# A two-layer diffusion block on one core: later loads at the start, value products of attention in threes, and one sum moved inside a scan

## The chip, the core and the metric

The kernel runs on one core of a Trainium2 chip, as one program. Its engines have a queue of instructions each and meet by semaphores: TensorE (PE, with its weight loads shown as PEld), VectorE (DVE), ScalarE (ACT), GpSimd (POOL) and SyncE (SP), which issues the DMAs. The metric is the device time of one execution in microseconds (us); the median of 3 runs before the change is 2692.45 us (2690.4 to 2694.46).

## The reference, cut to what matters

Two layers work on 2048 latent tokens of width 1024, with 256 context tokens as a prefix. Each layer's input is modulated by a shift and a scale that come from a conditioning vector:

```
mod = (silu_c @ w_ada[l] + b_ada[l])[:, None, :]
q, k, v, g_a, xb, b_g, c_g, g_b = split_cols(modulate(x, shift, scale) @ w_in, widths)   # layer 0
q, zf, zb, i, g = split_cols(modulate(x, shift, scale) @ w_in, widths)                    # layer 1
```

Layer 0 has windowed attention (8 query heads on 2 key heads; a block of 128 queries sees all 256 context keys and the 384 latent keys around it, and a sink) beside a gated short convolution:

```
p = jax.nn.softmax(jnp.concatenate([sink_l, s_ctx, s_loc], axis=-1), axis=-1)
return (jnp.einsum('bkgij,bjkd->bikgd', p[..., 1:1 + lc], vc)
        + jnp.einsum('bkgij,bjkd->bikgd', p[..., 1 + lc:], v_n))
```

Layer 1 is a gated linear recurrence in two directions, 8 heads, computed in chunks:

```
S_t = diag(f_t) S_{t-1} + k_t v_t^T ,   o_t = S_t^T q_t
```

All is float32; the products of the projections are made of two halves, a rounded one and the rest, three matmuls for each block of 128 rows of the weight.

## The kernel before, in words

**Projections.** `proj` (L370) makes one block of 128 output channels for a group of 256 or 512 tokens: 8 steps of three matmuls (L377 to L379), each with a weight tile of 128 x 128 of its own and 256 or 512 columns. Layer 0 goes over the tokens in three passes. In each, `emit` takes the blocks one after another; a block's weights come by `wload` (L282), which loads 512 KB into one of three buffers `w`, and are split into two halves on ACT (L252) and DVE (L255). At the first pass the halves are also written back to memory for the later passes.

**The start.** Before any projection the modulation of layer 0 is made by `ada` (L179): 16 loads of 512 KB into the six buffers `wh`, each followed by four matmuls that fill a quarter of the array's columns each (L190). The inputs are transposed on PE (L313). Two blocks, the keys' and the values', are worked off as soon as each quarter of the modulation is there; their weights are loaded among the modulation's (`first_w`, L570). When the values' block is done, `ab_rest` (L596) asks for the mask and sink tables and queues the transposes of the other tokens (`transposed`, L355). A scheduler orders the whole program: each engine's queue is made from the instructions' dependences and its own clock, so an instruction may come much earlier in a queue than its line. `issue_after` gives a load an earlier instruction that it has to follow in the queue.

**Attention.** It is side work, `attend` (L792), put between the projections' matmuls. For a unit of one or two query blocks it makes the scores, the softmax, and then the products with the values: the probabilities are transposed on PE (L886) into a PSUM bank `pm`, ACT copies a bank into a buffer `pt` (L888), and matmuls that fill 64 of the 128 columns each, one half for each of two heads (L894), add them up in one bank `pa`. There are two banks `pm` and four buffers `pt`. A bank takes two blocks of 128 queries for each head, so a unit of two query blocks needs five banks; L876 takes them two at a time: two banks of transposes, their products, two more, their products, the fifth, its products.

**The scan.** Layer 1's `levels` (L1193) makes a head's scores by doubling the block length: seven levels, in each a copy of the keys on ACT (L1236), matmuls that fill 32 columns each (L1279), and products on DVE (L1242, L1245). Before the first level, eight matmuls against a constant 0/1 pattern (L1220, 32 columns each too) sum the products within pairs of neighbours, from an array that DVE has made (L1207 to L1211), and ACT copies the result (L1223). There are three PSUM banks `ps` for scores and levels.

A `yield` with a number gives the side work's cost; `Side.step` spends a budget on it in proportion to the projections.

Of the kernel before, what the change touches and what calls it, by code (L numbers as in the profile page):

```python
# [21 lines left out]
ALU = mybir.AluOpType  # L22
# [3 lines left out]
P = 128  # L26
# [28 lines left out]
class Kern:  # L55
# [226 lines left out]
    def wload(self, v, tag="wh", bank="pj", key=None):  # L282
        if key in self.kept:
            return self.wback(key)[0] + (bank,)
        raw = self.t("w", [P, KC, P])
        self.last = self.nc.sync.dma_start(raw, v)
        if tag != "pt":
            hl = self.split(raw, tag=tag)
            if key is not None:
                self.wkeep(key, hl)  # L290
            return hl + (bank,)

        q = [self.split(raw[:, i:i + 4, :], (P, 4, P), tag) for i in (0, 4)]
        return Halves(*[x[0] for x in q]), Halves(*[x[1] for x in q]), bank
# [301 lines left out]
    def ab_rest(self):  # L596

        with self.tc.issue_after(self.last.ins):
            self.tables_ab()
        self.shared = True  # L600
        self.first = self.last
        for t in range(4, NT):
            self.side.add(self.transposed(self.io["x"][0, t * P:(t + 1) * P, :], self.xT[:, :, (t - 4) * P:(t - 3) * P]))
# [69 lines left out]
    def wcols(self, a, *to, key=None):  # L673
        return self.wload(self.io["w_in_ab"][a // P], *to, key=key)
# [117 lines left out]
    def attend(self, b, ts, qv, sv):  # L792
# [83 lines left out]
        for b0 in range(0, len(banks), 2):  # L876
            todo = []
            for bank in banks[b0:b0 + 2]:
# [12 lines left out]
            for s, q0, d, o, n in todo:  # L891
# [301 lines left out]
    def levels(self, r, scores):  # L1193
# [8 lines left out]
        if scores:  # L1202
# [7 lines left out]
            nc.vector.tensor_tensor(own, own, q, ALU.mult)  # L1210
# [3 lines left out]


            Sd = self.t("Sd", [P, nt, 32])
            ps = self.ps("ps")
            for row in range(2):
                for j in range(0, P, 32):
                    nc.tensor.matmul(ps[j:j + 32, :n // 4], self.alt[:, row:row + 32],  # L1220
                                     cap(on, row * n + j, [(P, nt), (2, 16), (n + 1 - 2 * row * n, 2)]),
                                     start=(row == 0), stop=(row == 1))
            nc.scalar.copy(Sd, ps[:, :n // 4].rearrange("p (i t) -> p i t", t=32))  # L1223
            Sc = self.t("Sc", [P, n])
            r["A"], r["Sc"] = A, Sc
            yield 1.0
# [4 lines left out]
        for li, m in enumerate(LEVELS):  # L1231
            nb = n // (2 * m)
            if scores and li:

                X = self.t("X", [P, n])
                nc.scalar.copy(cap(X, 0, [(2 * m, nb), (m, 2), (1, m)]), cap(K, 0, [(2 * m, nb), (n + m, 2), (1, m)]))  # L1236
                self.level(m, X, A, Sd, Sc)
# [23 lines left out]
        r["T"] = td  # L1261

# [423 lines left out]
```

## Time and profile before

| what | value |
|---|---|
| median of 3 runs | 2692.45 us |
| profiled execution | 2695.45 us, of which the span from its first to its last instruction is 2693.7 us |
| PE busy | 2648.5 us (98%), 21556 matmuls |
| PEld busy | 2228.5 us (83%) |
| DVE, ACT, POOL busy | 1665.1, 1232.3, 43.1 us |
| DMA | 427.39 MB, mean 159 GB/s |
| mean granted TensorE clock | 0.993 |
| chain that ended last, by engine | PE 93%, DMA 3%, DVE 2%, ACT 1% |

PE is busy nearly all the time. Busy is not the same as useful: the ends of matmuls are modelled, and a matmul that is shown at 0.28 us can be followed by the next after 0.12 us. What a matmul costs is the distance from its start to the next one's start, and this is how the rows of the timeline are read below.

### The profile page before, as it was taken

Reading aid. Unit: us, or ns where it says so; the run is one execution under the profiler, and the core shown is the slowest. Engines: PE = TensorE matmul, PEld = TensorE weight load, DVE = VectorE, ACT = ScalarE, POOL = GpSimd, SP = SyncE. Lnnn points to the kernel's source line nnn. Section 1 sums busy time; section 2 is a strip of 40 time slices with the busy share of each in tenths; the row PEclk is TensorE's granted clock in tenths of the full one; section 3 lists DMA queues with packets and bytes.
Section 4 is the critical chain, followed back from the end, with each engine's and each line's share of the span. In section 5 each row is a group of like instructions: output and inputs, shape, how many; then the busy total and the mean of one; then the engine's idle time right before and its main releaser. Section 6 shows DMA issues by size and latency. Waiting matters only on the chain.

```text
span 2693.7 us, 53732 instructions
## 1 busy us (share of the span) xinstructions
PE 2648.5 (98%) x21556; PEld 2228.5 (83%) x21556; DVE 1665.1 (62%) x4075; ACT 1232.3 (46%) x2827; POOL 43.1 (2%) x160
## 2 busy tenths in 40 slices
PE   8999999999999999999999999999999999999998
PEld 5978888888888878889888888888978888887786
DVE  5556664455445467788756565658666555566776
ACT  4555544446455562136544444445344445444300
POOL 0000000000000000000000000000000000000000
PEclk8999999999999999999999999999999999999999
DMA  8955544334333346655543443435344432335433
GB/s 333 314 190 182 199 166 139 118 126 144 136 131 136 114 150 193 202 166 188 181 162 137 146 153 119 157 131 183 142 167 146 154 107 103 126 111 197 147 141 110
DMA packets 201620, 427.39 MB, mean 159 GB/s; under 512 B 15910, under 2 KB 93467, under 8 KB 201371
## 3 DMA queue, kind: packets, MB, share of 16 engines
q1 hardware_dynamic: 201370, 423.96, 45.8%
q8 instruction: 170, 2.79, 0.4%
q14 instruction: 80, 0.65, 0.1%
HBM read 278.13 MB, written 145.76 MB: 157 GB/s over the span
## 4 chain that ended last, share of the span: by engine, by line
PE 93%; DMA 3%; DVE 2%; ACT 1%; issue 0%; SPq 0%; DVEq 0%; ACTq 0%
PE pj L377 17%; PE pj L378 17%; PE pj L379 17%; PE pj L505 4%; PE pj L507 4%; PE pj L506 4%; PE pa L894 3%; PE pm L886 3%; PE pm L1384 3%; PE pj L1145 2%; PE pj L1146 2%; PE pj L1144 2%; PE ps L1279 2%; PE ps L1309 2%; PE pm L1298 1%; PE ps L1220 1%
## 5 line engine op out<-in xcount | busy, mean ns | idle before, releaser
L377 PE MATMUL pj<-xa,wh 128*128 128x512 f32 x1120 | 444.3, 397 | 0.3 <-ACT gl L1130 0.3
L378 PE MATMUL pj<-xa,wh 128*128 128x512 f32 x1120 | 443.9, 396 | 0.0
L379 PE MATMUL pj<-xa,wh 128*128 128x512 f32 x1120 | 442.3, 395 | 0.0
L379 PEld LDWEIGHTS pj<-xa,wh 128*128 128x128 f32 x1120 | 210.6, 188 | 44.1 <-issue 2.5
L378 PEld LDWEIGHTS pj<-xa,wh 128*128 128x128 f32 x1120 | 210.8, 188 | 41.5 <-issue 2.7
L377 PEld LDWEIGHTS pj<-xa,wh 128*128 128x128 f32 x1120 | 210.6, 188 | 41.4 <-issue 0.9
L1236 ACT COPY X<-gl 128x512 f32<-128x512 f32 x192 | 115.4, 631 | 149.0 <-PE ps L1279 80.0
L377 PE MATMUL pj<-xb,wh 128*128 128x256 f32 x608 | 175.6, 289 | 0.7 <-ACT acc L237 0.7
L378 PE MATMUL pj<-xb,wh 128*128 128x256 f32 x608 | 174.1, 286 | 0.0
L379 PE MATMUL pj<-xb,wh 128*128 128x256 f32 x608 | 174.1, 286 | 0.0
L255 DVE TENSOR_TENSOR wh<-w,wh 128x1024 fp32r<-128x1024 f32 x98 | 119.7, 1221 | 66.6 <-ACT wh L252 57.5
L888 ACT COPY pt<-pm 128x512 f32<-128x512 f32 (+1 forms) x168 | 91.9, 579 | 142.8 <-PE pm L886 142.3
L1242 DVE TENSOR_TENSOR gl<-gl,xb 128x512 f32<-128x512 f32 (+1 forms) x240 | 149.0, 632 | 7.8 <-ACT X L1236 6.3
L1245 DVE TENSOR_TENSOR A<-A,xb 128x512 f32<-128x512 f32 x192 | 131.2, 686 | 33.6 <-PE ps L1279 33.1
L252 ACT CAST wh<-w 128x1024 fp32r<-128x1024 f32 x98 | 102.1, 1049 | 107.1 <-PE pj L378 81.2
L377 PE MATMUL pj<-kb,wh 128*128 128x512 f32 (+1 forms) x384 | 140.0, 365 | 3.9 <-ACT gl L1130 3.4
L378 PE MATMUL pj<-kb,wh 128*128 128x512 f32 (+1 forms) x384 | 138.9, 362 | 0.0
L497 ACT CAST wh<-wh 128x1024 fp32r<-128x1024 f32 (+2 forms) x36 | 35.9, 997 | 224.7 <-DMA wh<-yT_ab 98.1
L379 PE MATMUL pj<-kb,wh 128*128 128x512 f32 (+1 forms) x384 | 138.3, 360 | 0.0
L826 DVE CUSTOM_DVE_ANT_0 ps<-ps,am,c_sink 128x384 f32<-128x384 f32 (+1 forms) x128 | 76.6, 603 | 93.4 <-PE ps L823 80.4
L377 PEld LDWEIGHTS pj<-xb,wh 128*128 128x128 f32 x608 | 115.8, 190 | 5.9 <-issue 2.7
L837 ACT ACTIVATE p<-ps,sm 128x256 f32<-128x256 f32 x144 | 68.3, 475 | 109.0 <-DVE sm L834 105.7
(384 smaller groups left out, 6553.1 us busy)
## 6 DMA issues: line engine op xcount, KB each, us to landing
wh<-w_parts SPq DMA_DIRECT2D x180, 512.0 KB
w_parts<-wh SPq DMA_DIRECT2D x148, 512.0 KB
w<-in_w_in_c SPq DMA_DIRECT2D x48, 512.0 KB
w<-in_w_ada SPq DMA_DIRECT2D x32, 512.0 KB
w<-in_w_in_ab SPq DMA_DIRECT2D x28, 512.0 KB
wh<-yT_ab SPq DMA_DIRECT2D x18, 512.0 KB
w<-x1T SPq DMA_DIRECT2D x18, 512.0 KB
wh<-in_w_ada SPq DMA_DIRECT2D x16, 512.0 KB
```

What stands on the lines that cost most here:

```text
L252: nc.scalar.copy(hi, raw)
L255: e.tensor_tensor(lo, raw, hi[:].bitcast(F32), ALU.subtract)
L377: nc.tensor.matmul(p[:, :N], hi[:, k, :], xh, start=(k == 0), stop=False)
L378: nc.tensor.matmul(p[:, :N], hi[:, k, :], xl, start=False, stop=False)
L379: nc.tensor.matmul(p[:, :N], lo[:, k, :], xh, start=False, stop=(k == KC - 1))
L505: nc.tensor.matmul(p, r["hi"][:, k, :], wh[:, s], start=(k == 0), stop=False)
L506: nc.tensor.matmul(p, r["hi"][:, k, :], wl[:, s], start=False, stop=False)
L507: nc.tensor.matmul(p, r["lo"][:, k, :], wh[:, s], start=False, stop=(k == KC - 1))
L888: nc.scalar.copy(d[:, :, 0:o], pt.rearrange("p (h c) -> p h c", h=2)[:, :, 0:o])
L1236: nc.scalar.copy(cap(X, 0, [(2 * m, nb), (m, 2), (1, m)]), cap(K, 0, [(2 * m, nb), (n + m, 2), (1, m)]))
L1242: nc.vector.tensor_tensor(kk, kk, cap(pt_, po + 1, [(pd - 1, 2), (2, nb), (0, m)]), ALU.mult)
L1245: nc.vector.tensor_tensor(aa, aa, cap(pt_, po + pd + 1, [(-pd - 1, 2), (2, nb), (0, m)]), ALU.mult)
```

## The change

It has three parts. The loads of weights for blocks other than the first two, the tables and the first token loads are held behind the last load of the modulation. Attention takes its banks three at a time instead of two, and goes through their products in reversed order, the last transposed first. In the scan the sums within pairs, and the DVE product that they need, move into the step of the first scored level.

```
-    def wload(self, v, tag="wh", bank="pj", key=None):
+    def wload(self, v, tag="wh", bank="pj", key=None, after=None):
...
-        self.last = self.nc.sync.dma_start(raw, v)
+        with self.tc.issue_after(after.ins) if after else ExitStack():
+            self.last = self.nc.sync.dma_start(raw, v)
...
     def ab_rest(self):
-        with self.tc.issue_after(self.last.ins):
+        with self.tc.issue_after(self.ada_last.ins):
             self.tables_ab()
         self.shared = True
-        self.first = self.last
+        self.first = self.ada_last
...
     def wcols(self, a, *to, key=None):
-        return self.wload(self.io["w_in_ab"][a // P], *to, key=key)
+        return self.wload(self.io["w_in_ab"][a // P], *to, key=key, after=None if to else self.ada_last)
...
-        for b0 in range(0, len(banks), 2):
+        for b0 in range(0, len(banks), 3):
             todo = []
-            for bank in banks[b0:b0 + 2]:
+            for bank in banks[b0:b0 + 3]:
...
-            for s, q0, d, o, n in todo:
+            assert not first or (todo[-1][1] == 0 and todo[-1][4] == nt * P)
+            for s, q0, d, o, n in reversed(todo):
...
-            nc.vector.tensor_tensor(own, own, q, ALU.mult)
...
-            ps = self.ps("ps")
-            for row in range(2):
-                for j in range(0, P, 32):
-                    nc.tensor.matmul(ps[j:j + 32, :n // 4], self.alt[:, row:row + 32],
...
-            nc.scalar.copy(Sd, ps[:, :n // 4].rearrange("p (i t) -> p i t", t=32))
...
-            yield 1.0
...
                 nc.scalar.copy(cap(X, 0, [(2 * m, nb), (m, 2), (1, m)]), cap(K, 0, [(2 * m, nb), (n + m, 2), (1, m)]))
+                if li == 1:
+                    nc.vector.tensor_tensor(own, own, q, ALU.mult)
+                    self.within(on, Sd)
                 self.level(m, X, A, Sd, Sc)
...
+    def within(self, on, Sd):
+        nc = self.nc
+        n = on.shape[-1]
+        nt = n // P
+        ps = self.ps("ps")
+        for row in range(2):
+            for j in range(0, P, 32):
+                nc.tensor.matmul(ps[j:j + 32, :n // 4], self.alt[:, row:row + 32],
+                                 cap(on, row * n + j, [(P, nt), (2, 16), (n + 1 - 2 * row * n, 2)]),
+                                 start=(row == 0), stop=(row == 1))
+        nc.scalar.copy(Sd, ps[:, :n // 4].rearrange("p (i t) -> p i t", t=32))
```

Where it moves instructions, the queues show it. First PE's queue in layer 0's attention, before: `pa_1925` is the accumulator of one unit, `pt_` its copied banks, `pj_` a projection that runs beside it.

```order
L377 MATMUL pj_2127<-xa_247,wh_2087 128x512
L894 MATMUL pa_1925<-pt_1927,vc_548 64x256 x2
L886 MATMUL pm_1944<-c_ident,p_1784 128x128
L894 MATMUL pa_1925<-pt_1934,v_582 64x256 x2
L886 MATMUL pm_1944<-c_ident,p_1784 128x128
L886 MATMUL pm_1944<-c_ident,p_1785 128x128 x2
L886 MATMUL pm_1985<-c_ident,p_1785 128x128 x2
```

The products of the first two banks stand here, with a transpose between them. The same unit (now `pa_1897`) in PE's queue after the change:

```order
L379 MATMUL pj_2243<-xa_370,wh_2209 128x512
L897 MATMUL pa_1897<-pt_1941,v_582 64x256 x2
L897 MATMUL pa_1897<-pt_1934,v_582 64x256 x2
L897 MATMUL pa_1897<-pt_1899,vc_548 64x256 x2
L888 MATMUL pm_1958<-c_ident,p_1784 128x128 x2
L888 MATMUL pm_1958<-c_ident,p_1785 128x128 x2
L380 MATMUL pj_2243<-xa_369,wh_2211 128x512
```

Three banks' products now stand together, the last copied bank first, and nothing is between them. In the whole queue the products form 132 unbroken runs before and 68 after, of 416 instructions in both. (The profile counts each of these float32 matmuls twice, so 832, and a row with x2 here is a row with x4 there.)

The second place is SP's queue in the start, before: `wh_` are the modulation's loads, `w_` weights of later blocks, `kb_588` tokens, `cs_` tables of the rotation.

```order
L188 DMA wh_334<-in_w_ada 128x1024
L286 DMA w_621<-in_w_in_ab 128x1024
L188 DMA wh_343<-in_w_ada 128x1024
L360 DMA kb_588<-in_x 128x1024
L188 DMA wh_349<-in_w_ada 128x1024
L286 DMA w_742<-in_w_in_ab 128x1024
L286 DMA w_850<-in_w_in_ab 128x1024
L188 DMA wh_382<-in_w_ada 128x1024
L188 DMA wh_388<-in_w_ada 128x1024
L188 DMA wh_397<-in_w_ada 128x1024
L188 DMA wh_403<-in_w_ada 128x1024
L683 DMA cs_495<-in_k_cos 128x512
```

After the change, SP's queue from the same load on:

```order
L188 DMA wh_334<-in_w_ada 128x1024
L188 DMA wh_343<-in_w_ada 128x1024
L188 DMA wh_349<-in_w_ada 128x1024
L188 DMA wh_382<-in_w_ada 128x1024
L188 DMA wh_388<-in_w_ada 128x1024
L188 DMA wh_397<-in_w_ada 128x1024
L188 DMA wh_403<-in_w_ada 128x1024
L685 DMA cs_495<-in_k_cos 128x512
L686 DMA cs_496<-in_k_sin 128x512
L164 DMA am_584<-in_k_amask 128x384
L166 DMA c_sink<-in_sink_ab 128x8
L361 DMA kb_588<-in_x 128x1024
```

Three weight loads, one token load and the two tables have moved behind the modulation's last load; `w_621`, `w_742` and `w_850` follow right behind these rows.

The third place is PE's queue in the scan, one pair of a head's two token groups, before: `kst_` holds the products to be summed, `A_` and `X_` are a level's operands.

```order
L1144 MATMUL pj_15207<-wh_15199,xa_12137 128x256
L1220 MATMUL ps_15112<-kst_15098,c_alt 32x128 x8
L1145 MATMUL pj_15207<-wh_15201,xa_12137 128x256
L1146 MATMUL pj_15207<-wh_15199,xa_12138 128x256
L1144 MATMUL pj_15207<-wh_15199,xa_12137 128x256
```

The same sum after the change (L1147 to L1149 are the values' projections, L1267 the sums, L1288 a level):

```order
L1147 MATMUL pj_15230<-wh_15222,xa_12137 128x256
L1267 MATMUL ps_15122<-kst_15098,c_alt 32x128 x8
L1288 MATMUL ps_15132<-A_15100,X_15119 32x32 x16
L1148 MATMUL pj_15230<-wh_15224,xa_12137 128x256
L1149 MATMUL pj_15230<-wh_15222,xa_12138 128x256
```

The sum that stood alone is now followed by the first level of its token group. Over the whole queue, sums and levels together form 131 unbroken runs before and 132 after.

## Rows read from the trace of the kernel before

**Rows 1.** Windows: PE, PEld, DVE, ACT, POOL busy us (instructions); clock; DMA share, GB/s
```profile
0.00:26.80 26.80, 15.98 (x111) 9.21 (x111) 9.89 (x29) 7.23 (x12) 0.83 (x9) 0.92 0.90 342
26.80:60.70 33.90, 32.67 (x209) 24.01 (x210) 23.01 (x50) 16.84 (x29) 0.00 (x0) 0.86 0.91 343
60.70:943.00 882.30, 879.96 (x5585) 734.61 (x5585) 469.94 (x1248) 462.22 (x1134) 23.34 (x79) 1.00 0.47 162
```
**Rows 2.** Timeline, PE, one run of four value products: start us, us, what, shapes
```profile
208.85 0.28 PE L377 MATMUL pj<-xb,wh 128*128 128x256 f32 x1
208.97 0.28 PE L378 MATMUL pj<-xb,wh 128*128 128x256 f32 x1
209.18 0.65 PE L894 MATMUL pa<-pt,vc 128*64 128x256 f32 x4
209.77 0.38 PE L379 MATMUL pj<-xb,wh 128*128 128x256 f32 x1
209.99 0.28 PE L377 MATMUL pj<-xb,wh 128*128 128x256 f32 x1
```
**Rows 3.** Timeline, PE, one run of eight value products
```profile
183.48 0.28 PE L379 MATMUL pj<-xb,wh 128*128 128x256 f32 x1
183.69 1.08 PE L894 MATMUL pa<-pt,vc 128*64 128x256 f32 x8
184.71 0.39 PE L377 MATMUL pj<-xb,wh 128*128 128x256 f32 x1
184.93 0.28 PE L378 MATMUL pj<-xb,wh 128*128 128x256 f32 x1
```
**Rows 4.** Timeline, PE, four value products with transposes behind them
```profile
485.81 0.40 PE L378 MATMUL pj<-xa,wh 128*128 128x512 f32 x1
486.05 0.39 PE L379 MATMUL pj<-xa,wh 128*128 128x512 f32 x1
486.37 0.65 PE L894 MATMUL pa<-pt,vc 128*64 128x256 f32 x4
486.95 0.66 PE L886 MATMUL pm<-c_ident,p 128*128 128x128 f32 x4
487.37 0.48 PE L377 MATMUL pj<-xa,wh 128*128 128x512 f32 x1
487.68 0.40 PE L378 MATMUL pj<-xa,wh 128*128 128x512 f32 x1
```
**Rows 5.** Timeline, PE, two transposes between projections
```profile
407.09 0.38 PE L886 MATMUL pm<-c_ident,p 128*128 128x128 f32 x2
407.22 0.36 PE L377 MATMUL pj<-xb,wh 128*128 128x256 f32 x1
407.42 0.28 PE L378 MATMUL pj<-xb,wh 128*128 128x256 f32 x1
```
**Rows 6.** Waits of PE, whole span: for what; us in total, times, longest
```profile
PE pm L886 <- ACT p L855: 0.6, 2, 0.3
```
**Rows 7.** Groups by form: ACT's copy of a bank; busy us, mean ns; idle before
```profile
L888 ACT COPY pt<-pm 128x512 f32<-128x512 f32 x160 | 89.3, 589 | 137.4 <-PE pm L886 136.9
```
**Rows 8.** Line L188, the modulation's loads: who waited for them (us, times)
```profile
  PEld ps L190: 0.5, 2
```
**Rows 9.** Timeline, PE, the last wait for tokens in the start
```profile
26.76 1.54 PE L313 MATMUL pm<-c_ident,kb 128*128 128x128 f32 x6 [0.53 <-DMA kb<-in_x]
```
**Rows 10.** Timeline, SP's queue, the modulation's last four loads: start, us
```profile
29.76 7.35 SPq L188 DMA_DIRECT2D wh<-in_w_ada  x4
```
**Rows 11.** Windows of the start, columns as in rows 1
```profile
20.00:30.00 10.00, 7.23 (x38) 4.39 (x39) 4.50 (x10) 3.90 (x6) 0.00 (x0) 0.62 1.03 403
30.00:40.00 10.00, 10.00 (x59) 7.29 (x58) 6.50 (x15) 4.14 (x6) 0.00 (x0) 0.70 1.03 409
```
**Rows 12.** Lines L1210 and L1223 in the scan: ns min/median/max, first and last start
```profile
L1210 DVE TENSOR_TENSOR kst<-kst,Q x32: 674/684/693, 1320.5 to 2451.8; 128x512 f32<-128x512 f32 x32
L1223 ACT COPY Sd<-ps x32: 245/267/272, 1325.9 to 2459.2; 128x128 f32<-128x128 f32 x32
```

More of the change, by code (lines that the diff above doesn't have):

```diff
@@ L1216, in levels @@
             Sd = self.t("Sd", [P, nt, 32])
-            ps = self.ps("ps")
-            for row in range(2):
-                for j in range(0, P, 32):
-                    nc.tensor.matmul(ps[j:j + 32, :n // 4], self.alt[:, row:row + 32],
-                                     cap(on, row * n + j, [(P, nt), (2, 16), (n + 1 - 2 * row * n, 2)]),
-                                     start=(row == 0), stop=(row == 1))
-            nc.scalar.copy(Sd, ps[:, :n // 4].rearrange("p (i t) -> p i t", t=32))
             Sc = self.t("Sc", [P, n])
             r["A"], r["Sc"] = A, Sc
-            yield 1.0
         prod = (F, 0, n)
```

## The prediction

> **What bounds the kernel.** I read the page's busy shares first, then the windows by stage, then PE's timeline start by start, then the waits. PE is busy 98% of the span and makes 93% of the chain that ended last, so the time is PE's queue from end to end, and what counts is what each instruction takes from that queue. The windows [rows 1] say where PE is not full: in the first 26.8 us it works 15.98; from there to the first ordinary block at 60.7 it works 32.67 of 33.9; from 60.7 to 943 us, the stage with the attention, 879.96 of 882.3. In that stage no other engine reaches 60% and the DMA share is 0.47. So there is next to nothing to win from waits there (2.3 us in 882), and a gain can only come from PE doing the same work in fewer microseconds. PE's timeline shows where such time hides. A projection of 256 columns takes 0.12 us from start to start (208.85 to 208.97). When a run of value products comes between, the steps before and behind it are longer [rows 2]: 208.97 to 209.18 is 0.21, and 209.77 to 209.99 is 0.22. That is time shown as busy in which PE does no more work.
>
> **Part 1: attention in threes.** No instruction is added or removed: PE's queue has the same 832 value products and 656 transposes, ACT the same 168 copies. What changes is how they stand together: 132 unbroken runs of value products before, 68 after. Two causes: by the code there were 100 groups (three for each of 28 two-block latent units, two for each of four units of one block with three banks, one for each of eight others) and now there are 68; and before, the scheduler slid transposes or projections into groups 32 times, for which the reversed order leaves no room, because the first product of a group now needs its last copy.
>
> The price of a run. Four products [rows 2]: from 208.97 to 209.99 is 1.02 us, less two ordinary steps of 0.12, so 0.78 us. Eight products [rows 3]: from 183.48 to 184.93 is 1.45, less 0.24, so 1.21 us. Two runs of four cost 1.56, one of eight 1.21: joining saves 0.35 us. With transposes behind the run [rows 4]: 486.05 to 487.68 is 1.63, less two projection steps of 0.24 (485.81 to 486.05) and four transposes; a pair of transposes between projections costs 0.33 less one step of 0.12 [rows 5], so 0.21, and four 0.42. That leaves 0.73 for the four products, 0.05 less than in rows 2, so I put joining there at 0.30 (an estimate: it takes the same 0.05 off the fixed part). In the new queue 43 of the 68 runs have transposes behind them. I take 0.32, with 0.30 and 0.35 as ends: 64 x 0.32 = 20.5 us, ends 19.2 and 22.4. All of it lies on the path, since the stage is PE's from start to end. The transposes themselves may be spread among the projections, as they now are more often, at no cost: the 0.21 us of a pair [rows 5] is just two steps of 0.105.
>
> What is added is a wait. The first product of a group stands in PE's in-order queue behind nothing but its semaphore, and needs the copy made last; the third bank's transposes need a bank `pm` back, of which there are two. A copy takes 589 ns [rows 7]. Behind a waiting product stands everything on PE. In the new queue 30 or so projections stand between a group's last transposes and its first product, which at 0.12 to 0.23 us each is some 4 to 6 us, ten times a copy. In the trace PE's transposes waited 0.6 us in all [rows 6] with the same two banks, and the products do not appear among the waits. I put this wait at 0, its bounds at -0.6 (those waits gone) and, were every one of the 68 groups to wait a whole copy, +40 us; I take the value of the row.
>
> The Trainium skill has two rules here that disagree. "TensorE: Matmul & The Clock Gate" (Part 2, What happens when you issue a matmul) says that one matmul's drain overlaps the next one's fill, so that a step costs just its columns; "TensorEngine Tiling (Array Packing)" (Tiling Modes, Key Properties) says that changing the tiling mode drains the engine. By the first alone joining runs would save nothing and the sum would be the start's term alone; by the second each of the 64 runs that go is a drain on the way in and one on the way out, without a price. The 0.09 and 0.10 us that the neighbours of a run lose [rows 2] side with the second.
>
> **Part 2: loads behind the modulation.** On SP six loads and two small ones move behind the modulation's last. Of the loads, four of 512 KB and the mask table of 192 KB stood between modulation loads. At the 403 to 409 GB/s of this stretch [rows 11], 2.29 MB are 5.6 us: that is what the last modulation load could gain if DMA set its time. It does not: from 26.8 us on PE is full, and in the whole start it waited for modulation weights 0.5 us, in two pieces [rows 8]; there are six buffers `wh`, so the later loads wait themselves for PE to free one, and SP spends 7.35 us on the last four [rows 10]. PE's order up to the first ordinary block is nearly the same before and after. The one wait for DMA that shows late, 0.53 us for tokens [rows 9], has the mask table ahead of it in the queue: 192 KB, 0.5 us earlier. With what PE idles up to 60.7 us (1.2 us behind 26.8, [rows 1]) I take -1 us, bounds 0 and -5.6. The moved weights are not needed before the first ordinary block at 60.7 us; all that moved is 2.3 MB more behind the last modulation load, issued by 37.1 [rows 10], so they land by about 46 (an estimate from the same rate) and are split on ACT and DVE by 50.
>
> TensorE's clock is at 1.2 GHz for part of 20 to 40 us, after PE had idled (0.62 and 0.70 of full speed over these two windows, [rows 11]): 20 us at a mean of 0.66 is about 13.6 us at half speed. The work in it can start half a microsecond earlier, no more, so I leave the loss as it is and put 2 us either way into the range.
>
> **Part 3: sums in the first scores' step.** PE's count is the same, and the runs of narrow matmuls in the scan are 131 before and 132 after: 22 sums now touch a level where 16 did, but more levels stand alone. One run more is +0.3 us by the price above. On DVE the product (684 ns) and on ACT the copy of the sums (267 ns) move from before the first level to its second step [rows 12], 32 times; PE is full there and other work covers them. Only where the last heads' levels are exposed, at the ends of the two passes (three pairs), could the 0.95 us show: 3 x 0.95 = 2.9 us, on either side, since the chain loses at its start what it gets later. I take +0.3.
>
> **Sum.** -20.5 - 1 + 0.3 = -21.2 us. The profiled execution took 2695.45 us (2693.7 in the span, 1.75 around it) and would take 2674.2; it was 3.0 us above the median of the runs, so by the median 2692.45 - 21.2 = 2671.2 us. I say 2671.
>
> What else moves: each joined group gives back 0.8 of side budget and each scan 1.0, so the side work runs a little ahead. The queue shows little of it: the last value product stands behind 3812 of 10560 projection matmuls, before behind 3931. The boundaries between stages, where PE waits now, are dealt anew; I put 5 us either way into the range for that.
>
> **Rivals.**
> 1. The start is DMA's after all: if the modulation's last load comes 5.6 us earlier and all behind it follows, the start gives 5.6 instead of 1, and the time is 2666. For it: the DMA share in the start is 0.90 or more [rows 1]. Against it: the 0.5 us of waits [rows 8]. 10%.
> 2. The new wait (slower): PE stops at groups until ACT has copied the last bank, with every projection behind. It decides from 21.2 / 68 = 0.31 us a group on; at a whole copy of 0.589 us it is 40 us, and 2692.45 - 21.2 + 40 = 2711. For it: the reversed order asks for the newest copy first, and ACT has casts of 1 us in its queue. Against it: 30 projections in between. 5%.
> 3. Joining is free of gain: if the lost steps around a run are only drawn longer, nothing changes but the start: 2691. It is what the first of the two rules above gives (the Trainium skill, "TensorE: Matmul & The Clock Gate", Part 2). For it: ends of matmuls are modelled. Against it: I use starts alone, and two timeline places agree. 4%.
> 4. Half of the gain returns as waits at 68 joined groups or at the stage boundaries: 2681. For it: denser side work asks ACT for its copies in shorter time. 6%.
>
> My forecast has the remaining 75%.
>
> **How the numbers follow.** The likeliest case's own range is -19.2 to -22.4 for the runs, 0 to -2 for the start, 0 to +3 for the scan, 5 us of boundaries and 2 of clock: about 2664 to 2678. The range that should hold 8 in 10 reaches to rival 1 below and rival 4 above: 2662 to 2682. A measurement of this kernel can tell about 0.2%, 5.4 us, from no change. Faster by more: the forecast, rivals 1 and 4, less a little for rerolled boundaries, 0.90. Within: rival 3 and small parts of the others, 0.05. Slower: rival 2, 0.05.
>
> **What would show it.** In the changed kernel's profile: busy PE in the attention's stage down by some 20 us with the same count of instructions (so the windows of that stage end some 20 us earlier), not less idle time; runs of 8 and 16 value products in PE's timeline with one long step before and one behind; the first ordinary block starting at about 59.7 us instead of 60.7; the scan's stage as long as before. Wrong would be: waits of PE for L890 (the copy of a bank) of some microseconds; the first ordinary block at 56 us or earlier; an attention stage as long as before.

## The result, and the profile after

| | before | changed |
|---|---|---|
| median of the runs | 2693.45 us (4 runs, 2690.4 to 2698.88) | 2665.94 us (4 runs, 2662.65 to 2669.1) |
| ratio, 95% interval | | 0.9896 [0.9874, 0.9917] |
| profiled execution, span | 2695.45, 2693.7 us | 2669.1, 2667.3 us |
| PE busy | 2648.5 us | 2624.7 us |
| unbroken runs of value products | 132 | 68 |

The kernel became 27.5 us faster, where 21.2 were forecast. Run once more, in another set of runs, it stood at 0.9901 [0.9887, 0.9914], which is 26.7 us. The time, 2666, lies inside the range and 5 us under the number. One of the six runs of the sums alone, below, took 8005 us at full clock for no cause that is known; its median counts that run, its ratio does not.

To see where it went I cut PE's queue at the same work in each kernel: the start (up to the first ordinary block), the middle (from there through the first 4704 ordinary projection matmuls: the attention and the output that follows it) and the rest (the scan and all behind it). The last lines of the table are the parts run alone, told below.

| span of PE, us | start | middle | rest | last matmul ends |
|---|---|---|---|---|
| before | 60.7 | 1175.5 | 1448.0 | 2684.2 |
| changed | 57.4 | 1162.5 | 1438.0 | 2657.9 |
| changed, run again | 58.1 | 1158.5 | 1440.0 | 2656.6 |
| threes alone | 58.7 | 1158.5 | 1448.9 | 2666.1 |
| sums alone | 58.0 | 1174.8 | 1439.0 | 2671.8 |
| loads alone | 58.6 | 1174.1 | 1448.1 | 2680.8 |

The middle gave 13 to 17 us, the rest 8 to 10, the start 3. The two profiles of the changed kernel differ by 4 us in the middle: TensorE was at half speed there for 13.7 us in the first and for 6.8 in the second, which makes 3.4 of the 4. The windows at these cuts show what kind of time went. First before, the middle and the rest (columns as in [rows 1]):

```profile
60.73:1236.21 1175.48, 1166.69 (x7107) 972.11 (x7106) 693.84 (x1758) 572.48 (x1337) 23.34 (x79) 1.00 0.50 167
1236.21:2684.24 1448.03, 1433.12 (x14134) 1223.12 (x14132) 932.47 (x2223) 635.75 (x1450) 18.90 (x72) 1.00 0.42 145
```

The changed kernel, the same work:

```profile
57.38:1219.90 1162.52, 1148.77 (x7108) 977.41 (x7107) 698.57 (x1758) 571.87 (x1337) 23.02 (x79) 0.99 0.51 170
1219.90:2657.90 1438.00, 1430.12 (x14134) 1224.60 (x14132) 928.20 (x2223) 633.27 (x1450) 26.03 (x72) 1.00 0.42 146
```

The counts of instructions are equal to within one. In the middle PE is busy 17.9 us less and idle 5.0 us more (13.75 against 8.79). In the rest it is the other way: 3.0 us less busy, and 7.0 us less idle (7.88 against 14.91). Two different things happened: in the middle the same matmuls became cheaper, behind it PE waits less.

What the new groups look like is in PE's timeline of the changed kernel, one run of 16:

```profile
405.46 0.39 PE L380 MATMUL pj<-xa,wh 128*128 128x512 f32 x1
405.68 0.39 PE L378 MATMUL pj<-xa,wh 128*128 128x512 f32 x1
406.00 1.09 PE L897 MATMUL pa<-pt,v 128*64 128x256 f32 x12
406.92 0.60 PE L897 MATMUL pa<-pt,vc 128*64 128x256 f32 x4
407.45 0.66 PE L888 MATMUL pm<-c_ident,p 128*128 128x128 f32 x4
```

One long step stands before the 16 (405.68 to 406.00, 0.32, where the one before it took 0.22), and the last four take 0.53 up to the transposes behind them (406.92 to 407.45), where four in the middle of a run take 0.43 (the 0.43 by which [rows 3] are longer than [rows 2]). Between them the products follow one another without idle time; by the single starts the rest of the price lies in the step behind the first pair of products (0.26 us where later pairs take 0.21) and in the second step behind the group (0.17 where 0.11 is usual).

PE's weight loads (PEld) show what is special at the two ends. In the kernel before, beside [rows 2]:

```profile
208.74 0.19 PEld L377 LDWEIGHTS pj<-xb,wh 128*128 128x128 f32 x1
208.86 0.19 PEld L378 LDWEIGHTS pj<-xb,wh 128*128 128x128 f32 x1
209.18 0.20 PEld L894 LDWEIGHTS pa<-pt,vc 128*64 128x64 f32 x4
209.76 0.19 PEld L379 LDWEIGHTS pj<-xb,wh 128*128 128x128 f32 x1 [0.39 <-issue]
209.87 0.19 PEld L377 LDWEIGHTS pj<-xb,wh 128*128 128x128 f32 x1
```

Among projections a step's weights are loaded while the step before it runs (208.74 for the matmul at 208.85, 208.86 for the one at 208.97). The load of the first product begins at 209.18, with the product itself, and the load of the projection behind the run at 209.76, with the matmul at 209.77. At both ends of a run no load runs ahead.

There is no wait for the copies: the changed kernel has no row of PE waiting for L890 (the copy, 588 ns as in [rows 7]), and the transposes' wait of [rows 6] is gone too. The idle time that the middle gained is in the output's stage behind the attention. PE's waits between 880 and 1110 us, changed kernel (us in total, times, longest):

```profile
PE pj L506 <- ACT ka L252: 3.6, 2, 2.1
PE pj L506 <- DVE A L520: 2.4, 1, 2.4
PE pj L506 <- DVE w L520: 0.6, 1, 0.6
```

Before, the same stage shows 0.4 us of such waits:

```profile
PE pj L505 <- DVE w L519: 0.4, 1, 0.4
```

The side work is done earlier now (the last value product starts at 985 us, before at 1034, while the first output matmul moved by 15 only), so less may be left to lie beside the casts for the output (L252) and DVE's residual sums (L520). That this exposes them is not shown: in two kernels below the last value product stands almost where it did (twos in reversed order, behind projection 3932) or still earlier than here (threes in the old order, behind 3788), and 3.0 and 2.6 us of such waits come in them.

### The profile page after: what moved, and what is told of

Same layout as the page of the kernel before. It is cut to its first block, busy times and chain, and to the rows that moved or that the text cites. A ratio compares the mean times of both kernels' runs of the same rounds, so it can differ in the third digit from the quotient of the medians.

```text
span 2667.3 us, 53718 instructions
## 1 busy us (share of the span) xinstructions
PE 2624.7 (98%) x21556; PEld 2233.5 (84%) x21556; DVE 1665.5 (62%) x4075; ACT 1229.1 (46%) x2827; POOL 49.9 (2%) x160
## 4 chain that ended last, share of the span: by engine, by line
PE 95%; DMA 3%; DVE 1%; ACT 1%; issue 0%; SPq 0%; DVEq 0%; ACTq 0%
PE pj L378 18%; PE pj L380 18%; PE pj L379 18%; PE pj L506 4%; PE pj L508 4%; PE pj L507 4%; PE pa L897 3%; PE pm L888 3%; PE pj L1147 3%; PE pj L1148 3%; PE pm L1393 3%; PE ps L1288 3%; PE pj L1149 3%; PE ps L1318 2%; PE pm L1307 1%; PE ps L1267 1%
## 5 line engine op out<-in xcount | busy, mean ns | idle before, releaser
L252 ACT CAST wh<-w 128x1024 fp32r<-128x1024 f32 x98 | 102.6, 1049 | 124.9 <-PE pj L379 96.1
L890 ACT COPY pt<-pm 128x512 f32<-128x512 f32 (+1 forms) x168 | 91.5, 578 | 120.5 <-PE pm L888 114.4
L378 PEld LDWEIGHTS pj<-xb,wh 128*128 128x128 f32 x608 | 115.9, 191 | 6.4 <-DVE sg L789 1.7
L379 PEld LDWEIGHTS pj<-xb,wh 128*128 128x128 f32 x608 | 115.9, 191 | 2.6 <-issue 1.5
```

The source lines that it names most:

```text
L252: nc.scalar.copy(hi, raw)
L378: nc.tensor.matmul(p[:, :N], hi[:, k, :], xh, start=(k == 0), stop=False)
L379: nc.tensor.matmul(p[:, :N], hi[:, k, :], xl, start=False, stop=False)
L890: nc.scalar.copy(d[:, :, 0:o], pt.rearrange("p (h c) -> p h c", h=2)[:, :, 0:o])
```

## The experiments

Each kernel is the one before with the edit shown, unless said otherwise. Times are medians of the runs, the difference is the ratio to the kernel before with its 95% interval, turned into us.

| run | median, us | ratio | against before, us |
|---|---|---|---|
| e1_threes | 2674.55 | 0.9935 [0.9922, 0.9947] | -17.5 [-21.0, -14.3] |
| e2_loads | 2692.02 | 0.9999 [0.9991, 1.0008] | -0.3 [-2.4, 2.2] |
| e3_sums | 2684.94 | 0.9968 [0.9956, 0.998] | -8.6 [-11.8, -5.4] |
| e4_threes_fwd | 2693.61 | 1.0007 [0.9998, 1.0017] | 1.9 [-0.5, 4.6] |
| e5_sums_stay | 2686.89 | 0.9981 [0.9972, 0.999] | -5.1 [-7.5, -2.7] |
| e6_sums_keep | 2689.27 | 0.9991 [0.9982, 1.0] | -2.4 [-4.8, 0] |
| e7_twos_rev | 2685.96 | 0.9974 [0.9964, 0.9984] | -7.0 [-9.7, -4.3] |
| e8_fives | 2717.16 | 1.0097 [1.0082, 1.0113] | 26.1 [22.1, 30.4] |
| e9_after_again | 2665.94 | 0.9901 [0.9887, 0.9914] | -26.7 [-30.4, -23.2] |
| e10_threes_sums | 2666.87 | 0.9905 [0.9892, 0.9919] | -25.6 [-29.1, -21.8] |
| e11_fewer_cr | 2728.05 | 1.0131 [1.0116, 1.0147] | 35.3 [31.2, 39.6] |
| e12_fives_w | 2680.21 | 0.9953 [0.9941, 0.9966] | -12.7 [-15.9, -9.2] |

**Threes alone**

```diff
-        for b0 in range(0, len(banks), 2):
+        for b0 in range(0, len(banks), 3):
-            for s, q0, d, o, n in todo:
+            for s, q0, d, o, n in reversed(todo):
```

> The kernel before with part 2 alone: attention's banks in threes, the products of a group issued in reversed order. PE's queue then has 68 unbroken runs of value products instead of 132. Theory A (each run costs PE a fixed 0.32 to 0.35 us): the stage up to the last value product ends 20 to 22 us earlier, and the whole kernel is 13 to 22 us faster, since the next stage may take back up to 7 us as idle time of PE. Rival B (the gain of the change came from the scan's and the start's parts): 0 to 5 us faster. Rival C (all parts of the 27 us hang on this one, because the boundaries behind it fall better): 25 to 30 us faster.

It came out as theory A says. Middle and rest in its windows:

```profile
58.71:1217.20 1158.49, 1145.90 (x7107) 975.34 (x7106) 696.33 (x1758) 571.93 (x1337) 23.17 (x79) 1.00 0.50 169
1217.20:2666.10 1448.90, 1435.48 (x14134) 1226.03 (x14132) 932.20 (x2223) 635.54 (x1450) 18.78 (x72) 1.00 0.42 145
```

The middle is 17.0 us shorter: 20.8 us less busy, 3.8 more idle. The rest is as long as before, so this part gains nothing in the scan, and rivals B and C are out.

**Threes in the old order**

```diff
-        for b0 in range(0, len(banks), 2):
+        for b0 in range(0, len(banks), 3):
```

> The kernel before with attention's banks in threes, but the products of a group issued in the old order, oldest copy first. The groups are as few as in the changed kernel, but the scheduler slides transposes and projections into them: 131 unbroken runs of value products in PE's queue against 132 before and 68 in the changed kernel. Theory A (what costs is each run in the queue, 0.32 to 0.35 us): within 2 us of the kernel before. Rival B (what gains is the larger group in the code, by fewer steps of the planner or fewer waits for copies): 13 to 22 us faster, like threes with reversed products.

Theory A again: groups of three without the reversed order keep 131 runs, and gain nothing. What pays is the run that stays unbroken in PE's queue, not the group in the code.

**Twos in reversed order**

```diff
-            for s, q0, d, o, n in todo:
+            for s, q0, d, o, n in reversed(todo):
```

> The kernel before with attention's banks in twos as they were, but the products of a group in reversed order, so nothing can slide into a group: 100 unbroken runs of value products against 132 before and 68 in threes. Theory A (the price is 0.32 to 0.35 us a run): 32 runs fewer, 9 to 12 us faster. Rival B (threes gained through the place where the attention ends, which moves from 3931 to 3812 main matmuls only there, and here stays): within 3 us. Rival C (all of the gain of threes comes from the order): 15 to 19 us faster.

The gain lies between B and A; A's lower end of 9 is inside the interval. The price itself held. I took for each run the distance from the start of the step before it to the start of the second step behind it, less two ordinary steps and 0.107 us for each 256 columns of its products ([rows 2] and [rows 3] differ by 0.43 us in four such products), and added up the runs of a trace: 44.9 us for 132 runs before, 44.4 for the 131 in the old order, 34.4 for these 100, 22.5 for 68, 14.4 for the 40 of the last experiment below. That is 0.33 to 0.36 us a run throughout, and 10.5 us less for the 32 runs that went here. The middle became only 7.5 us shorter in its profile: by its window PE is busy 9.9 us less and idle 2.4 more.

```profile
57.44:1225.40 1167.96, 1156.80 (x7107) 972.10 (x7105) 695.94 (x1758) 570.97 (x1337) 24.35 (x79) 1.00 0.50 168
```

**Loads alone**

```diff
-        self.last = self.nc.sync.dma_start(raw, v)
+        with self.tc.issue_after(after.ins) if after else ExitStack():
+            self.last = self.nc.sync.dma_start(raw, v)
```

> The kernel before with part 1 alone: the loads that the first two blocks don't need go behind the modulation's weights. Theory A (the clock: PE idles a little less early on and the half-speed stretch is 6.8 us long instead of 13.7): the first ordinary block starts at about 57.4 instead of 60.7 us, and the kernel is 2 to 4 us faster; TensorE's granted clock between 20 and 40 us is higher than before. Rival B (the shorter half-speed stretch in the changed kernel was chance, or comes with other parts): the first ordinary block at 59.7 to 60.7 us, the kernel 0 to 1 us faster. Rival C (DMA sets the start): the start is shorter by up to 5.6 us at the same clock.

The time shows no gain: -0.3 us, with 2.4 either way. Rival C's 5.6 us are out, theory A's 2 to 4 lie at the edge of the interval or beyond it, and rival B's 0 to 1 us fits. The profiled execution does start its first ordinary block at 58.6 us, but so do the kernels whose loads were left alone (58.7 with threes, 58.0 with sums). What differs most is how long TensorE ran at the lower of its two clocks, and that differs from one execution to the next. Windows of 20 to 30 and 30 to 40 us with the loads moved:

```profile
20.00:30.00 10.00, 8.07 (x41) 5.29 (x42) 5.01 (x10) 4.28 (x7) 0.00 (x0) 0.60 1.03 408
30.00:40.00 10.00, 10.00 (x71) 6.96 (x70) 6.55 (x16) 2.87 (x5) 0.00 (x0) 0.89 0.79 267
```

and with the loads as before, sums moved:

```profile
20.00:30.00 10.00, 7.28 (x48) 4.50 (x41) 5.51 (x11) 4.05 (x7) 0.00 (x0) 0.69 1.00 392
30.00:40.00 10.00, 10.00 (x77) 7.20 (x76) 7.53 (x17) 3.98 (x6) 0.00 (x0) 0.97 1.03 413
```

Half speed lasts (0.40 + 0.11) x 20 = 10.2 us in the first, (0.31 + 0.03) x 20 = 6.8 in the second, 13.6 in [rows 11]. The profiled execution of before had the longest of all traces here. The changed kernel, one and the same, had 6.8 us in one profile and 10.2 in the other, with the first ordinary block at 57.4 and 58.1. The move is seen in the DMA column (267 against 413 GB/s behind 30 us), and little in PE's waits. For tokens (`in_x`) PE waits behind 20 us 1.3 us before, in two pieces, of which [rows 9] shows the later; the earlier is the first line here. The changed kernel has one wait of 0.50, the second line:

```profile
25.58 0.66 PE L313 MATMUL pm<-c_ident,kb 128*128 128x128 f32 x2 [0.77 <-DMA kb<-in_x]
25.87 1.54 PE L314 MATMUL pm<-c_ident,kb 128*128 128x128 f32 x6 [0.50 <-DMA kb<-in_x]
```

With the loads alone it is 0.3 us, with threes alone 1.2, with the sums alone 1.5. Where half speed lasts equally long, the kernels with the loads moved (and three buffers `w`) reach their first ordinary block about half a microsecond earlier (at 6.8 us of half speed 57.3, 57.3 and 57.4 against 57.4, 57.8 and 58.0; at 10.2 us 58.1 and 58.6 against 58.5, 58.7, 59.2 and 59.4). So the move may be worth half a microsecond, which is less than these runs can tell.

**Sums alone**

```diff
-            nc.vector.tensor_tensor(own, own, q, ALU.mult)
...
-            yield 1.0
...
+                if li == 1:
+                    nc.vector.tensor_tensor(own, own, q, ALU.mult)
+                    self.within(on, Sd)
```

> The kernel before with part 3 alone: own times q and the sums inside two rows move from before the scan's first level into its second step. Runs of narrow matmuls in PE's queue: 132 against 131. Theory A (the scan and the tail are 10 us shorter in the changed kernel because this part takes a wait off the exposed ends of the passes): 7 to 11 us faster, PE's idle time behind the attention down by that much. Rival B (this part moves nothing by itself; the 10 us come from where the stages' boundaries fall after part 2): within 2 us of the kernel before. Rival C (the chain loses later what it gains at its start): 0 to 3 us slower.

Theory A: the rest is 9.0 us shorter with the old attention in front of it, so the gain behind the attention is this part's own. In the kernel before, all of PE's idle time in the rest lies between 2020 and 2530 us (the windows up to 2020 and from there):

```profile
1236.21:2020.00 783.79, 783.79 (x8330) 676.62 (x8329) 509.58 (x1115) 377.72 (x741) 18.90 (x72) 1.00 0.44 154
2020.00:2530.00 510.00, 495.10 (x5132) 420.90 (x5131) 310.77 (x838) 241.92 (x689) 0.00 (x0) 0.99 0.39 134
```

The gain lies there too: counted at the same projection matmuls, the kernel with the sums moved gains nothing in the rest up to 2020 us. PE's waits in the last scans and behind them show which. Before, 2230 to 2530 us:

```profile
PE pa L1451 <- ACT o L1450: 2.9, 2, 1.8
PE pj L505 <- DMA ka<-w_parts: 2.1, 1, 2.1
PE ps L1279 <- ACT X L1236: 1.3, 3, 0.8
PE pm L1384 <- ACT pm L1403: 1.1, 1, 1.1
PE ps L1279 <- DVE A L1245: 1.0, 3, 0.4
```

With the sums moved, 2223 to 2520 us:

```profile
PE pm L1390 <- ACT pm L1409: 1.8, 2, 1.1
PE pm L1439 <- DMA X<-q_back: 0.9, 1, 0.9
PE pa L505 <- DVE o L1462: 0.8, 1, 0.8
```

Gone are the levels' waits for the keys' copy and for DVE's product (1.3 and 1.0), the transposes' wait for the outputs (2.9) and the wait for parts of the weights (2.1). The very end shows one such place. The last level of the last scan before, in PE's timeline:

```profile
2485.30 0.63 PE L507 MATMUL pj<-ka,wh 128*128 128x512 f32 x1
2486.17 0.94 PE L1279 MATMUL ps<-A,X 128*32 128x64 f32 x32 [0.25 <-ACT X L1236]
2487.90 0.65 PE L1279 MATMUL ps<-A,X 128*32 128x64 f32 x32 [0.79 <-ACT X L1236]
```

and with the sums moved:

```profile
2472.40 0.40 PE L507 MATMUL pj<-xa,wh 128*128 128x512 f32 x1
2472.73 0.65 PE L1285 MATMUL ps<-A,X 128*32 128x64 f32 x32
```

Before, two pieces of 32 of the last level stand behind these projections, and both wait for the copy; now one stands ahead of the last projections, the other behind them, and neither waits. Part 3 does two things at once: it moves the sums and it takes a step out of each scan. The next two runs part them.

**One step fewer, the sums where they were**

```diff
             r["A"], r["Sc"] = A, Sc
-            yield 1.0
```

> The kernel before with one step fewer for each scan of scores: the sums inside two rows stay where they were, before the first level, but no step ends behind them, so the side work goes on to the first level at once. 130 runs of narrow matmuls in the scan's part of PE's queue against 131. Theory A (part 3 alone gained 7 us because a scan takes one step less of the side work's budget, so that the last scans of a pass have main projections left beside them): 5 to 8 us faster, PE's waits between the levels from 2240 us on gone. Rival B (it gained because the sums' product and copy went out of the head of the chain): within 2 us of the kernel before. Rival C (both are needed): 2 to 5 us faster.

**The sums moved, the step kept** (sums alone, and this)

```diff
             r["A"], r["Sc"] = A, Sc
+            yield 1.0
```

> The kernel before with the sums moved into the second step as in part 3, but with the step that ended behind them kept, so a scan takes as much of the side work's budget as before. 139 runs of narrow matmuls in the scan's part of PE's queue against 131 before and 132 with part 3 whole, 8 x 0.33 = 2.6 us more by the price of a run. Theory A (the budget's step gained): 0 to 4 us slower than the kernel before, its waits between the last levels as before. Rival B (the shorter head of the chain gained): 3 to 8 us faster.

Neither theory has it all: the step alone gives 5.1 us, the move alone 2.4. That the step gains by itself is clear of the noise; the move's interval reaches 0. How the 8.6 us of both divide is not settled. By the medians of the same sets of runs it is 5.9 and 3.5, and 7.0 for both; in the profiles the rest is 6.7 us shorter with one step fewer, 5.8 with the move, 9.0 with both. They take different waits away. With one step fewer (2230 to 2530 us) the transposes wait 0.4 for the outputs instead of 2.9, but the wait for parts of the weights and those of the levels for the keys' copy are still there:

```profile
PE pj L505 <- DMA ka<-w_parts: 2.1, 1, 2.1
PE ps L1278 <- ACT X L1235: 1.3, 2, 0.7
PE pa L1450 <- ACT o L1449: 0.4, 1, 0.4
```

With the sums moved and the step kept it is the other way round: no level waits for the keys' copy, the wait for the parts is down to 0.3, and the transposes still wait 1.3 for the outputs:

```profile
PE pm L1391 <- ACT pm L1410: 1.8, 2, 1.1
PE pa L1458 <- ACT o L1457: 1.3, 1, 1.3
PE pm L1440 <- DMA X<-q_back: 0.9, 1, 0.9
```

The move gains although this kernel has 139 runs of narrow matmuls in the scan against 131. The very end shows the difference too. With one step fewer and the sums where they were, both pieces of the last level still wait for the keys' copy; with the sums moved and the step kept (the last line) the end is as with the sums alone:

```profile
2474.91 1.08 PE L1278 MATMUL ps<-A,X 128*32 128x64 f32 x32 [0.70 <-ACT X L1235]
2476.64 1.08 PE L1278 MATMUL ps<-A,X 128*32 128x64 f32 x32 [0.64 <-ACT X L1235]
2478.48 0.65 PE L1286 MATMUL ps<-A,X 128*32 128x64 f32 x32
```

So the end is the move's doing. Why one step fewer shortens the rest stays open. It does not simply bring the scans forward: I counted the projection matmuls that stand ahead of each scan's last level matmul (every 192nd in PE's queue), and with one step fewer 13 of the 32 come earlier, by up to 20 projection matmuls, 6 later, by up to 34, and 13 where they were.

**The changed kernel again, and without its loads.** The second leaves out part 1 of the change; its diff against the changed kernel is the one under "Loads alone", taken back.

> The changed kernel once more, beside the runs below. Theory A (the parts add up: threes -17.4, loads 0, sums -7.0 us, each run alone against the kernel before): 23 to 27 us faster than the kernel before. Rival B (the parts help one another, since the first pair of results stood at -27.5): 28 to 31 us faster.

> The kernel before with part 2 and part 3, the loads left where they were. Theory A (the loads do nothing): the same time as the changed kernel within 2 us, 22 to 28 us faster than the kernel before. Rival B (the loads bring their 3 us only where the other parts are in): 3 us or more slower than the changed kernel.

Theory A in both by the numbers; in the first the interval reaches into rival B's 28 to 31 as well. The parts alone add up to -17.5 - 0.3 - 8.6 = -26.4, the whole gives -26.7, and without the loads it is -25.6. The two differ by 1 us, inside either interval.

**Fives: can more be had?** The changed kernel, its two-block units in one group each; a buffer `pt` more, and for its room fewer of the buffers `cr` and `cg`. By the code these hold no tables: `keep` puts into them the queries and gates that a head pair carries from one pass over the tokens to the next, one of each for each of four pairs.

```diff
-        for b0 in range(0, len(banks), 3):
+        for b0 in range(0, len(banks), 5):
-   ... cr=4, cg=4, p=4, pt=4 ...
+   ... cr=3, cg=2, p=4, pt=5 ...
+            todo.reverse()
+            if first:
+                todo.sort(key=lambda x: not (x[1] == 0 and x[4] == nt * P))
```

> The changed kernel with attention's banks in fives, which is a whole two-block unit: one group a unit, the full-width product first, one buffer more for the copied banks, and for its room one buffer fewer of the rotations' cr and two fewer of cg. 40 unbroken runs of value products in PE's queue against 68, with 10 to 20 products each. Theory A (the price of a run holds on): 28 x 0.33 = 9 us faster than the changed kernel, 34 to 37 us faster than the kernel before. Rival B (a whole unit's copies, or fewer tables' buffers, make PE wait): no faster than the changed kernel, with PE waiting for the copy of a bank or for the rotations. Rival C (the attention then ends still earlier and the output stage takes it back as waits): 4 to 6 us faster than the changed kernel.

It was 26.1 us slower than the kernel before, and so 53 slower than the changed one, with PE waiting 26.6 us in the scores, for the exponentials. Two causes were mixed in it, and the next two runs part them.

**Fewer `cr` and `cg` in threes.** The changed kernel with `cr=3, cg=2` and nothing else.

> The changed kernel, attention's banks in threes, with one buffer fewer of the rotations' cr and two fewer of cg, as the kernel with fives had. Theory A (what made fives slow are the fewer buffers: the casts on GpSimd that fill cr wait for the previous unit's scores, and two units' scores come in a heap for which PE waits): 40 to 55 us slower than the changed kernel, PE waiting some 25 us in the scores for the exponentials and TensorE at half speed for some of it. Rival B (what made fives slow is the group of five itself): within 3 us of the changed kernel.

**Fives with room from the raw weights.** The changed kernel in fives as above, with `w=2` instead of 3, `cr` and `cg` left at 4.

> The changed kernel with attention's banks in fives, the room taken from the raw weights (two buffers instead of three) and cr and cg left at four each. 40 unbroken runs of value products against 68. Theory A (the price of a run holds on and two raw weight buffers are enough): 6 to 9 us faster than the changed kernel. Rival B (the group of five makes the scores wait, whatever the buffers): 40 us or more slower than the changed kernel, with the same waits as in the first kernel with fives. Rival C (two raw weight buffers make PE wait for weights): slower, with waits for the weights instead of the scores.

The buffers were it: with threes and fewer of them the kernel is 62 us slower than the changed one, more than the 40 to 55 of theory A. Which of the two buffers it is was not tried. How they make the scores wait is not shown either: the casts that fill `cr` follow PE's scores in the changed kernel too. PE's waits, whole span, and its window from 330 to 760 us:

```profile
PE ps L812 <- ACT p L843: 22.5, 13, 2.9
```

```profile
330.00:760.00 430.00, 401.81 (x2419) 333.81 (x2418) 213.13 (x575) 199.47 (x498) 11.22 (x32) 0.93 0.36 125
```

The changed kernel is busy 429.50 of these 430 us at full clock. Here PE stops for 28.2 us, and at a mean clock of 0.93 it runs 2 x 0.07 x 430 = 60 us at half speed, which loses another 30: the clock doubles the price of the waits. With fives and all of `cr` and `cg` the scores' wait is absent, the copies of the banks show as small waits (1.1 us for the transposes, 0.2 for the products), and the runs cost 14.4 us where those of threes cost 22.5. The kernel is still 14 us slower than the changed one. Rival C has it: PE's largest waits there are for DVE's residual sums, which use the `w` buffers too, and for a weight's cast:

```profile
PE pj L506 <- DVE w L520: 7.4, 3, 4.5
PE pj L1149 <- ACT wh L252: 5.2, 1, 5.2
```

The rest, where no value product stands, is 1446.5 us there against 1438.0 and 1440.0 in the changed kernel. So joining more runs still takes its price off, 8 us, but on this kernel no room for the fifth buffer was found that costs less. Nothing run here beats the changed kernel.

## Why the prediction was right, and where it was not

**The attention: right.** The sum had 64 x 0.32 = 20.5 us on PE's busy time, and threes alone took 20.8 off it. The number of runs was the right thing to count: 131 gain nothing, 100 and 68 gain in proportion (9.9 and 20.8 us of PE's busy time). The long steps around a run are real time, so rival 3 is out. Of the two rules weighed, the runs side with the Trainium skill's "TensorEngine Tiling (Array Packing)" (Tiling Modes, Key Properties), where changing the mode drains the engine; the drain that overlaps the next fill, from the Trainium skill's "TensorE: Matmul & The Clock Gate" (Part 2, What happens when you issue a matmul), holds inside a run, where four products more cost 0.43 us, and not across its ends, 0.33 to 0.36 us for both. No run here tells a drain from a weight load that is held back: the rows of PEld show that at both ends the load does not run ahead.

**The wait added: right, at 0.** No product waits for its copy; rival 2 is out.

**What came back: inside the range, but at nothing in the sum.** The prediction let the boundaries between stages fall either way by 5 us. They gave back 3.8 us in threes alone and 2.4 in reversed twos, as waits of the output's matmuls for casts and residual sums. That is rival 4 at a fifth of the gain instead of a half. What brings these waits stays open: the last value product moved from behind projection 3931 to behind 3812 in threes, which would leave less side work beside the output, but in reversed twos it stands behind 3932 and the waits come as well.

**The start: right in size, but the trace after misleads.** -1 was said, -0.3 [-2.4, 2.2] measured, and about half a microsecond by the first ordinary blocks at equal half speed. The first ordinary block at 57.4 us, where it was at 60.7 and I had named 59.7, looks like a gain of 3 us by the changed loads; most of it is the clock's spread between executions. Rival 1 is out; that the time came to its 2666 us is chance.

**The sums: the term that was mis-sized.** +0.3 was said, within 2.9, and it measured -8.6. The step that failed is "PE is full there and other work covers them. Only where the last heads' levels are exposed, at the ends of the two passes (three pairs), could the 0.95 us show". I priced the two instructions that moved, and only where nothing covers them. From 1236 to 2020 us the sentence held, PE is never idle there; from there to 2530 us it is idle for 14.9 us, and that is where the gain lies. And the step between them goes too, in every one of the 32 scans. The two experiments give 5.1 us to the step alone and 2.4 to the move alone, with the division unsettled. My sign of being right, the scan's stage as long as before, failed: the rest is 1438 to 1440 us where it was 1448. In the prediction the step stands only as "each scan 1.0" of budget given back, and is judged by the place of the last value product, which lies in another layer and says nothing of the scan. The idle time was there to be read in the windows, with the waits of the last scans' levels among it, and I weighed neither.

**The sum.** By the measured parts: -17.5, -0.3 and -8.6. The forecast of -21.2 was right as to its main term, of which 3 us came back as waits, and short by the scan's 9. The two errors go against each other, so that the time lies as near as 5 us to the number is in part luck.

## What to carry to other kernels

Count the places where a matmul that fills half of the columns meets one that fills them all: each unbroken run of such matmuls cost 0.33 to 0.36 us here, whatever its length, and an order of issue that makes the first of a group depend on its newest input keeps a scheduler from breaking the run. A step in a planner's side work can be a cost of its own: taking one out of each of 32 scans was worth 5.1 us [2.7, 7.5] with no instruction moved by hand. And an earlier start of a block in one profiled execution is no evidence on the edit there until kernels with and without the edit have been compared at the same length of half speed.

## What the hardware showed that was not expected

The lower clock in the start lasted 13.6 us before and 6.8 with the sums moved, whose queue of PE is the same up to there, and the first ordinary block moved by 2.7 us with it. And with fewer `cr` and `cg`, waits of PE of 2.3 to 3.0 us, one or two at each of five places between 330 and 760 us, cost about twice their length: the 28.2 us of idle time there came with 60 us at half speed, which lose 30 more (mean granted clock 0.93, where the changed kernel has 1.00). Last, at the ends of a run of half-width products PE's weight load begins only with its own matmul, where among projections it runs one step ahead.
